# A hybrid decoder layer: the second x tile loaded in two parts, casts and two passes of squares moved to VectorE, and the order of k's and q's evacuations changed

## The chip, the cores and the metric

The kernel runs on one core of a Trainium2 chip. The metric is device time in microseconds (us) of one execution. The engines are named as in the profile: PE is TensorE's matmul (PEld its weight load), DVE is VectorE, ACT is ScalarE, POOL is GpSimd, SP is SyncE, which here only issues DMAs.

## What is computed

One layer of a decoder trunk on x of 1024 positions by 1024 channels, all in float32. What bears on the change is the head of it: the normalised input is projected to q, k and v, and q and k are normalised per head of 64 channels before a sliding-window attention.

```python
h = rmsnorm(x, mix_norm)                       # 1024 x 1024
q, k, v, su, sv, g_a, g_b = split(h @ w_in)    # q: 8 heads x 64; k, v: 2 heads x 64
q = rmsnorm(q, q_norm); k = rmsnorm(k, k_norm) # per head
scores = q @ k.T * 64 ** -0.5 + alibi          # window 128, blocks of 128 queries, sinks
y_att = softmax(scores) @ v
y_sgu = chunked_spatial_gating(su, sv, ...)
x = x + (sigmoid(g_a) * (y_att @ w_oa) + sigmoid(g_b) * (y_sgu @ w_ob)) @ w_out
x = x + conv_gated_mlp(rmsnorm(x, ffn_norm), ...)
```

## The kernel before

Every float32 product is made of three matmuls (`mm3`): each operand is split into a high part, rounded to TensorE's float32r, and a low part, the rest (`copy_hi` on ScalarE, then a subtraction on VectorE or GpSimd); high by high, high by low and low by high are summed in PSUM.

The head of the kernel, up to the first scores, is written out by hand: within `man = tc.manual_schedule()` each engine executes its instructions in the order of the program text, and TensorE does so throughout the kernel. Semaphores are put in by the framework. The stages are:

- A few matmuls of a tile of ones (`warm`, L230) keep TensorE busy while the first input arrives.
- `x_block(k)`, k = 0 to 7: x transposed comes from DRAM as eight tiles `xw[k]` of 128 channels by 1281 columns (one column of the norm's gain, 256 of k's and v's weights, 1024 positions). `xload` issues the loads on SP, tile 0 in two parts. ScalarE and VectorE write the high and low parts of the scaled positions (`x`, in halves of 512) and of the weights (`wkv`), and TensorE adds 24 matmuls to the two PSUM tiles `pkv`, which in the end hold k and v of all positions, positions on partitions.
- `wq_split(c)`: the weights of the first half of q's heads, two chunks of 128x1024, high part (L254) and low part (L255).
- `tsquare(t)`, t = 0 to 7: x comes a second time, by rows (`xt`, eight tiles of 128 positions by 1024 channels, `tload`), and the squares of each row are summed into column t of `ss8` (L219). All of `ss8` is needed for `eps_x` (L346) and `rstd` (L352), the reciprocal root of the rows' mean square. The input norm is so applied behind the projections; for q and k it drops out but for an epsilon, `eps_x`.
- `q_proj(n)`: 24 matmuls for 128 positions of four q heads, into a PSUM tile `pq` of pool H.
- Behind them: `q_sq`, squares of q; `q_ms`, their sums per head (L297, L298) and the power -1/2 on GpSimd (L299); `q_norm`, the product `qr` (L305); `q_trans`, two transposes on TensorE into `pqt` (L311); `q_split`, their high parts on ScalarE and low parts on VectorE (L320). For k: `ksq` and `kss` (L339, L340), `krs` (L347) and its power in two halves (L349, L403), `k_norm(h)`, the product `kr` (L356), `k_trans(h)`, four transposes into `pk` (L363), `k_hi` on ScalarE and `k_lo` on VectorE (L377) into kT, `k_twice`, a copy to the other half of the partitions. For v: `v_evac(h)` takes v out of `pkv` (L387), `v_split` splits it. `rms_rows` spreads `rstd` along rows by four matmuls with the identity (`rb`, L139) and copies it (`rstd_b`, L142).
- Then the attention: `s_mm(n)` makes the scores `sc` of 128 queries and four heads (L450, L453), `s_mask` adds the distance penalty (L466, L471), and TensorE is given other matmuls (`FILL`: later q groups, chunks of u and v of the gating unit) between.

Pool H has four PSUM tiles for `warm`, `pq`, `pk`, `pqt`, `rb` and later ones. A new tile takes the buffer whose last reader comes first in program order among those given back, and TensorE waits for that reader. The scores and `pkv` share another pool of two.

Of the kernel before, what the change touches and what calls it, by code (L numbers as in the profile page):

```python
# [13 lines left out]
AF = mybir.ActivationFunctionType  # L14
ALU = mybir.AluOpType
# [18 lines left out]
def build(tc, a):  # L34
    nc = tc.nc
    ctx = ExitStack()
    with ctx, tc.manual_schedule(engines={mybir.EngineType.PE}):
        body(ctx, tc, nc, a)


def body(ctx, tc, nc, a):
# [8 lines left out]
    def nm(s):  # L50
        uid[0] += 1
        return f"{s}_{uid[0]}"
# [15 lines left out]
    def Z(s, dt, shape, off=16):  # L68

        return late_by(zr[0], "Z", s, dt, shape, off)  # L70
# [8 lines left out]
    def PH(s):  # L79
        if psum.get("H") is None:  # L80
            return PS(s)[:, 0:512]
        return psum["H"].tile([128, 512], F, tag="H", name=nm(s))
# [4 lines left out]
    def copy_hi(dst, src, scale=1.0):  # L87
        return nc.scalar.activation(dst, src, AF.Copy, scale=scale)  # L88

    def mm3(out, wh, wl, mh, ml, first, last, **kw):  # L90

        nc.tensor.matmul(out, wh, mh, start=first, stop=False, **kw)  # L92
        nc.tensor.matmul(out, wh, ml, start=False, stop=False, **kw)  # L93
        nc.tensor.matmul(out, wl, mh, start=False, stop=last, **kw)  # L94
# [23 lines left out]
    mh05 = base.tile([128, 8], F, name="mh05")  # L118
    rstd = base.tile([128, 8], F, name="rstd")
# [14 lines left out]
    def rms_rows(pb, col, hs=(0, 1)):  # L134

        for h, p in zip(hs, pb):
            for s in range(4):
                c = 4 * h + s
                nc.tensor.matmul(p[:, s * 128:(s + 1) * 128], col[:, c:c + 1].to_broadcast([128, 128]), ident,  # L139
                                 start=True, stop=True)  # L140
        for h, p in zip(hs, pb):
            nc.scalar.copy(rstd_b[:, h * 512:(h + 1) * 512], p)  # L142
# [16 lines left out]
    wq = [Z("wq", R, (128, 2, 8, 256), 0)]  # L159
# [18 lines left out]
    def hx(j, k, c):  # L178

        h = c.start // 512  # L180
        return xq[k // 4][h][:, j, k % 4, c.start - 512 * h:c.stop - 512 * h]
# [14 lines left out]
    ss8 = at.tile([128, 8], F, name="ss8")  # L196
    pkv = [PS("pkv"), PS("pkv")]
    pk4 = [pkv[h].rearrange("p (s c) -> p s c", c=256) for h in range(2)]
    xr = {}
    x_first = [Y("xf", F, [128, 3, 1281]) for _ in range(2)]  # L200

    def xload(k):
        xr[k] = x_first[k // 3][:, k % 3, :] if k < 6 else pa.tile([128, 1281], F, tag="xr", name=nm("xr"), bufs=3)
        if k == 0:
            nc.sync.dma_start(xr[k][:, 0:513], a["xw"][k, :, 0:513])
            nc.sync.dma_start(xr[k][:, 513:1281], a["xw"][k, :, 513:1281])
        else:
            nc.sync.dma_start(xr[k], a["xw"][k])

# [6 lines left out]

    def tsquare(t):
        v = xt[t // 4][:, t % 4, :]
        nc.scalar.activation(v, v, AF.Square, accum_out=ss8[:, t:t + 1])  # L219

    man = tc.manual_schedule()
# [4 lines left out]
    nc.sync.dma_start(ident, a["ident"])  # L226
    nc.sync.dma_start(cp, a["cp"])
    warm = [PH("warm") for _ in range(4)]
    for i in range(11):
        nc.tensor.matmul(warm[i % 4][:, 0:128], rstd_b[:, 0:128], rstd_b[:, 0:128], start=True, stop=True)  # L230
    xcuts = {0: (slice(0, 256), slice(256, 512), slice(512, 1024))}

# [18 lines left out]
    def wq_split(c):  # L251
        rv = rwq[c].rearrange("p (k a) b -> p k (a b)", a=2)
        ks = slice(4 * c, 4 * c + 4)
        nc.scalar.activation(wq[0][:, 0, ks, :], rv, AF.Copy)  # L254
        nc.vector.tensor_tensor(wq[0][:, 1, ks, :], rv, wq[0][:, 0, ks, :].bitcast(F), op=ALU.subtract)  # L255

    x_block(0)
# [11 lines left out]
    x_block(7)  # L269
    wq_split(0)  # L270
    tsquare(0)
    tsquare(1)
    wq_split(1)
    for t in range(2, 6):
        tsquare(t)

    st = {}

    def q_proj(n):
        half, b = divmod(n, 8)  # L280
        w = wq[half]
        p = PH("pq")[:, 0:256]
        c = slice(b * 128, (b + 1) * 128)
        for k in range(8):
            mm3(p, hx(0, k, c), hx(1, k, c), w[:, 0, k, :], w[:, 1, k, :], k == 0, k == 7)
        st[("pq", n)] = p


    def q_sq(n):
        p = st.pop(("pq", n)).rearrange("p (h d) -> p h d", d=64)  # L290
        sq = qp.tile([128, 4, 64], F, tag="qsq", name=nm("qsq"), bufs=2)
        nc.scalar.activation(sq, p, AF.Square)
        st[("q", n)] = [p, sq]

    def q_ms(n):
        ss = qp.tile([128, 4], F, tag="qss", name=nm("qss"), bufs=4)
        nc.vector.tensor_reduce(ss, st[("q", n)][1], axis=AX.X, op=ALU.add)  # L297
        nc.vector.tensor_scalar(ss, ss, 1.0 / 64, eps_x[:, n % 8:n % 8 + 1], op0=ALU.mult, op1=ALU.add)  # L298
        nc.gpsimd.tensor_tensor(ss, ss, mh05[:, :4], op=ALU.pow)  # L299
        st[("q", n)][1] = ss  # L300

    def q_norm(n):
        p, ss = st.pop(("q", n))
        qr = st[("qr", n)] = qp.tile([128, 4, 64], F, tag="qr", name=nm("qr"), bufs=2)
        nc.vector.tensor_tensor(qr, p, ss.unsqueeze(2).to_broadcast([128, 4, 64]), op=ALU.mult)  # L305

    def q_trans(n):
        qr = st.pop(("qr", n)).rearrange("p h d -> p (h d)")
        p = PH("pqt")[:, 0:256]
        for t in range(2):  # L310
            nc.tensor.transpose(p[:, t * 128:(t + 1) * 128], qr[:, t * 128:(t + 1) * 128], ident)  # L311
        st[("qT", n)] = p

    def q_split(n):
        p = st.pop(("qT", n))
        qs = qp.tile([128, 2, 256], R, tag="qs", name=nm("qs"), bufs=2)
        for g in range(2):
            copy_hi(qs[ROWS[g], g, :], p[ROWS[g], :])
        for g in range(2):
            nc.vector.tensor_tensor(qs[ROWS[1 - g], g, :], p[ROWS[g], :], qs[ROWS[g], g, :].bitcast(F),  # L320
                                    op=ALU.subtract)
        st[("qT", n)] = qs
# [5 lines left out]
    krs = pa.tile([128, 16], F, name="krs")  # L328
# [3 lines left out]

    q_proj(0)
    q_proj(1)
    q_proj(2)
    ksqs = pa.tile([128, 8, 128], F, tag="sq", name="ksq")
    for h in range(2):
        ksq = ksqs[:, 4 * h:4 * h + 4, :]
# [1 line left out]
        nc.vector.tensor_reduce(kss[:, 8 * h:8 * h + 8], ksq.rearrange("p s (g d) -> p (s g) d", d=64),  # L340
                                axis=AX.X, op=ALU.add)
    tsquare(6)
    tsquare(7)
    nc.vector.tensor_scalar(kgq, cp[:, 184:185], cp[:, 185:186], -0.125, op0=ALU.mult, op1=ALU.mult)
    q_sq(0)
    nc.vector.tensor_scalar(eps_x, ss8, EPS / D, EPS * EPS, op0=ALU.mult, op1=ALU.add)  # L346
# [1 line left out]
                                   op0=ALU.mult, op1=ALU.add)  # L348
# [5 lines left out]
    def k_norm(h):  # L354
        ss = slice(4 * h, 4 * h + 4)
        nc.vector.tensor_tensor(kr[:, ss, :].rearrange("p s (g d) -> p s g d", d=64),  # L356
                                pk4[h][:, :, 0:128].rearrange("p s (g d) -> p s g d", d=64),
                                krs3[:, ss].unsqueeze(3).to_broadcast([128, 4, 2, 64]), op=ALU.mult)

    def k_trans(h):  # L360
        pk = PH("pk")
        for s in range(4):
            nc.tensor.transpose(pk[:, s * 128:(s + 1) * 128], kr[:, 4 * h + s, :], ident)  # L363
        st[("pk", h)] = pk

    def k_hi(h):
        cs = slice(512 * h, 512 * h + 512)
        pk = st[("pk", h)]
        for g in range(2):
            copy_hi(kTh[ROWS[g], g, cs], pk[ROWS[g], :], scale=kgq[ROWS[g], 0:1])  # L370

    def k_lo(h):
        cs = slice(512 * h, 512 * h + 512)
        pk = st.pop(("pk", h))
        for g in range(2):
            r = ROWS[g]
            nc.vector.scalar_tensor_tensor(kTl[r, g, cs], pk[r, :], kgq[r, 0:1], kTh[r, g, cs].bitcast(F),  # L377
                                           op0=ALU.mult, op1=ALU.subtract)

    def k_twice(h):  # L380
        cs = slice(512 * h, 512 * h + 512)
        for g in range(2):
            nc.scalar.copy(kTh[ROWS[1 - g], g, cs], kTh[ROWS[g], g, cs].bitcast(F))

    def v_evac(h):
        ss = slice(4 * h, 4 * h + 4)
        nc.vector.tensor_tensor(vt[:, ss, :], pk4[h][:, :, 128:256],  # L387
                                rstd[:, ss].unsqueeze(2).to_broadcast([128, 4, 128]), op=ALU.mult)

    def v_split():  # L390

        for g in range(2):
# [2 lines left out]
            copy_hi(vh_, vg_)  # L395
            nc.vector.tensor_tensor(vl_, vg_, vh_.bitcast(F), op=ALU.subtract)

    k_norm(0)
    k_trans(0)
    q_ms(1)  # L400
    q_norm(0)
    q_trans(0)
    nc.gpsimd.tensor_tensor(krs[:, 8:16], krs[:, 8:16], mh05, op=ALU.pow)  # L403
    q_norm(1)
    q_proj(3)
    q_sq(2)
    q_ms(2)
    nc.gpsimd.tensor_tensor(rstd, rstd, mh05, op=ALU.pow)
    nc.vector.tensor_scalar(nsink, sink_b, -1.0, None, op0=ALU.mult)
    k_hi(0)  # L410
    k_norm(1)
    q_split(0)
    k_lo(0)
    q_norm(2)
    q_trans(1)
    k_twice(0)
    rms_rows([PH("rb")], rstd, (0,))
    k_trans(1)
    q_sq(3)
    q_ms(3)  # L420
    v_evac(0)
    v_evac(1)
    copy_hi(u_next[0], u_raw[0])
    nc.gpsimd.tensor_tensor(u_next[1], u_raw[0], u_next[0].bitcast(F), op=ALU.subtract)
    q_split(1)
    rms_rows([PH("rb")], rstd, (1,))
    k_hi(1)
    k_lo(1)
# [1626 lines left out]
```

## Time and profile before

| what | us |
|---|---|
| median of 3 runs | 1177.23 |
| lowest and highest of them | 1176.56, 1178.11 |
| profiled execution | 1177.21 |
| span of its instructions | 1175.5 |
| TensorE busy in it | 1165.1 |
| first matmul of the first x block | 5.33 |
| first matmul of the first q group | 28.94 |
| first scores | 46.35 |

Times in the profile count from the start of the span. A timeline row gives the start, the duration of the merged group, engine, line and operation, the tile written and those read, shapes, the count, and in brackets the idle time of the engine ahead of it with what ended it. Where several instructions are merged (x2), the duration runs from the first start to the last end; neighbours on one engine overlap by up to 0.1 us. A row of the waits gives who waited for whom: us in total, times, longest. Lines are those of the kernel as printed above.

### The profile page before, as it was taken

The page shows a single profiled execution, that of the slowest core. Times are in us where ns is not written, and L with a number is a line of the kernel's source. Part 1 is how long each engine was busy: PE and PEld are TensorE (multiplying, and loading weights), DVE is VectorE, ACT ScalarE, POOL GpSimd, SP SyncE. Part 2 cuts the span into 40 slices and gives each one's busy share as a digit, 9 for nine tenths or more (in the row PEclk, how much of TensorE's full clock was granted, in tenths as well). Part 3 has the DMA queues.
Part 4 walks back from the last instruction along what each step waited for, and adds up shares of the span by engine and source line. Part 5 has one row for each costly group of instructions (what it writes and reads, how often), then busy time and mean ns, then how long its engine had stood idle before and what let it go on. Part 6 is the DMA issues. An engine that isn't in the chain of part 4 may idle for free.

```text
span 1175.5 us, 15803 instructions
## 1 busy us (share of the span) xinstructions
PE 1165.1 (99%) x5834; PEld 987.4 (84%) x5834; DVE 843.6 (72%) x974; ACT 565.5 (48%) x874; POOL 628.5 (53%) x434
## 2 busy tenths in 40 slices
PE   9999999999999999999999999999999999999998
PEld 9899999888888878888888888888888888888887
DVE  6677756743536876778788777887888787875674
ACT  7766568643436643334544444434444455425231
POOL 1567684598883863554877767676767640000000
PEclk9999999999999999999999999999999999999999
DMA  9210156256646763554554545454545268966471
GB/s 363 91 55 20 54 171 207 83 186 198 197 107 237 242 203 107 180 152 125 143 151 145 137 137 165 135 158 119 170 131 164 81 212 293 365 222 197 160 231 66
DMA packets 82093, 192.84 MB, mean 164 GB/s; under 512 B 9312, under 2 KB 16992, under 8 KB 81888
## 3 DMA queue, kind: packets, MB, share of 16 engines
q1 hardware_dynamic: 74160, 171.78, 42.3%
q0 software_dynamic: 7456, 15.73, 8.4%
q10 hardware_dynamic: 400, 4.33, 1.1%
q8 instruction: 46, 0.75, 0.3%
q14 instruction: 31, 0.25, 0.1%
HBM read 151.17 MB, written 49.02 MB: 170 GB/s over the span
## 4 chain that ended last, share of the span: by engine, by line
PE 85%; DVE 4%; ACT 3%; DMA 3%; POOL 2%; issue 1%; SPq 0%; DVEq 0%; POOLq 0%; ACTq 0%
PE pz L1068 48%; PE pd L1863 10%; PE pdy L1863 8%; PE px L94 2%; PE px L93 2%; PE px L92 2%; PE pu L94 1%; PE pu L92 1%; PE pu L93 1%; PE pv L525 1%; DMA xf<-xw 1%; PE pq L92 1%; PE pq L94 1%; PE pq L93 1%; DMA xt<-xt 1%
## 5 line engine op out<-in xcount | busy, mean ns | idle before, releaser
L1068 PE MATMUL pz<-T,qh 128*128 128x512 f32 x472 | 145.6, 390 | 0.0
L1068 PE MATMUL pz<-B,ph 128*128 128x512 f32 x352 | 109.6, 392 | 0.1
L1068 PEld LDWEIGHTS pz<-T,qh 128*128 128x128 f32 x472 | 88.4, 188 | 18.7 <-ACT u L893 0.3
L1027 POOL TENSOR_TENSOR pl<-lp,ph 128x1024 fp32r<-128x1024 f32 x30 | 75.2, 2505 | 53.1 <-ACT ph L88 53.1
L1068 PE MATMUL pz<-T,ql 128*128 128x512 f32 x236 | 91.8, 389 | 0.0
L1027 POOL TENSOR_TENSOR ql<-lq,qh 128x1024 fp32r<-128x1024 f32 x30 | 76.8, 2560 | 9.1 <-ACT qh L88 9.1
L1068 PEld LDWEIGHTS pz<-B,ph 128*128 128x128 f32 x352 | 65.2, 188 | 15.9 <-ACT x L1703 2.8
L1086 DVE TENSOR_TENSOR pz<-pz,rstd_b 128x1024 f32<-128x1024 f32 x60 | 73.9, 1232 | 4.5 <-ACT rstd_b L142 2.5
L1068 PE MATMUL pz<-T,s3h 128*128 128x512 f32 x232 | 71.4, 389 | 0.0
L1068 PE MATMUL pz<-y,wjh 128*128 128x512 f32 x224 | 69.5, 391 | 0.6 <-POOL y L1241 0.3
L1068 PE MATMUL pz<-B,pl 128*128 128x512 f32 x176 | 68.6, 390 | 0.0
L1863 PE MATMUL pd<-bh,ah 128*128 128x512 f32 x176 | 68.5, 389 | 0.0
L1863 PE MATMUL pd<-bl,ah 128*128 128x512 f32 x176 | 68.5, 389 | 0.0
L1863 PE MATMUL pd<-bh,al 128*128 128x512 f32 x176 | 68.5, 389 | 0.0
L1068 PE MATMUL pz<-B,AX 128*128 128x512 f32 x264 | 63.4, 389 | 0.0
L1068 PE MATMUL pz<-T,AX 128*128 128x512 f32 x264 | 63.4, 389 | 0.0
L1027 POOL TENSOR_TENSOR s3l<-lq,s3h 128x512 fp32r<-128x512 f32 x20 | 25.9, 1296 | 61.4 <-ACT s3h L88 61.4
L1068 PEld LDWEIGHTS pz<-T,AX 128*128 128x128 f32 x264 | 49.5, 188 | 10.3
L1068 PEld LDWEIGHTS pz<-B,AX 128*128 128x128 f32 x264 | 49.5, 188 | 10.3
L88 ACT ACTIVATE AX<-lr 128x1024 fp32r<-128x1024 f32 x22 | 23.4, 1064 | 69.9 <-POOL lr L629 69.9
L1558 DVE SCALAR_TENSOR_TENSOR tg<-pz,cp,tg 128x1023 f32<-128x1023 f32 (+1 forms) x44 | 56.3, 1278 | 0.8
L1558 DVE SCALAR_TENSOR_TENSOR tv<-pz,cp,tv 128x1023 f32<-128x1023 f32 (+1 forms) x44 | 56.2, 1278 | 0.8
(351 smaller groups left out, 3520.9 us busy)
## 6 DMA issues: line engine op xcount, KB each, us to landing
lp<-wup SPq DMA_DIRECT2D x22, 512.0 KB, 3.7
lq<-wup SPq DMA_DIRECT2D x22, 512.0 KB, 4.2
ra<-wdown SPq DMA_DIRECT2D x44, 256.0 KB, 4.8
b<-T SPq DMA_DIRECT2D x44, 256.0 KB, 3.7
lq<-wup POOLq DMA_DIRECT2D x42, 256.0 KB, 5.3
B<-tv SPq DMA_DIRECT2D x33, 256.0 KB, 2.1
T<-tt SPq DMA_DIRECT2D x33, 256.0 KB, 2.2
b<-B SPq DMA_DIRECT2D x33, 256.0 KB, 3.8
```

The costliest lines, as they stand in the source:

```text
L88: return nc.scalar.activation(dst, src, AF.Copy, scale=scale)
L92: nc.tensor.matmul(out, wh, mh, start=first, stop=False, **kw)
L93: nc.tensor.matmul(out, wh, ml, start=False, stop=False, **kw)
L94: nc.tensor.matmul(out, wl, mh, start=False, stop=last, **kw)
L525: nc.tensor.matmul(o, vhl[:, kb, g, :], w[:, 2 * g:2 * g + 2, :], start=i == 0 and g == 0, stop=i == len(ops) - 1, skip_group_check=True)
L1027: nc.gpsimd.tensor_tensor(l, r, h.bitcast(F), op=ALU.subtract)
L1068: nc.tensor.matmul(o, p[:, k, :], m, start=not more and k == 0 and j == 0, stop=k == nk - 1 and j == 2, skip_group_check=True)
L1086: nc.vector.tensor_tensor(z, z, rstd_b, op=ALU.mult)
L1558: nc.vector.scalar_tensor_tensor(t[:, j:], p[:, 0:1024 - j], cw[:, ci, 2 - j:3 - j], t[:, j:], op0=ALU.mult, op1=ALU.add)
L1863: nc.tensor.matmul(o[d], p[:, k - k0, m], q[:, k - k0, :], start=new and k == 0 and j == 0, stop=k == HK - 1 and j == 2, skip_group_check= ...
```

## The change

The second x tile is loaded in two parts, one with the gain, the weights and the first 512 positions, one with the rest. One warm matmul of eleven goes. The squares of row tiles 5 and 7 are taken by one `tensor_tensor_reduce` each on VectorE; the one of tile 7 stands right behind those of tiles 2 to 5 in program order, ahead of k's squares. The high part of q's weights is copied by VectorE. `q_proj(2)` goes behind `k_trans(0)`. The power of the second half of `krs` goes ahead of `k_norm(0)`, and so ahead of the power of `q_ms(1)`; that of `rstd` goes from behind `q_ms(2)` to behind `k_hi(0)`. `k_norm(1)`, `q_norm(1)`, both q transposes and `k_lo(0)` come ahead of `q_proj(3)`; `k_twice(0)`, both `v_evac`, `q_split(0)` and `q_split(1)` come ahead of `k_trans(1)` and of the first `rms_rows`, and so ahead of `q_ms(3)`.

```diff
         elif k == 1:
+            nc.sync.dma_start(xr[k][:, 0:769], a["xw"][k, :, 0:769])
+            nc.sync.dma_start(xr[k][:, 769:1281], a["xw"][k, :, 769:1281])
...
     def tsquare(t):
         v = xt[t // 4][:, t % 4, :]
+        if t in (5, 7):
+            nc.vector.tensor_tensor_reduce(out=v, in0=v, in1=v, scale=1.0, scalar=0.0, op0=ALU.mult, op1=ALU.add,
+                                           accum_out=ss8[:, t:t + 1])
+            return
         nc.scalar.activation(v, v, AF.Square, accum_out=ss8[:, t:t + 1])
...
-    for i in range(11):
+    for i in range(10):
         nc.tensor.matmul(warm[i % 4][:, 0:128], rstd_b[:, 0:128], rstd_b[:, 0:128], start=True, stop=True)
...
-        nc.scalar.activation(wq[0][:, 0, ks, :], rv, AF.Copy)
+        nc.vector.tensor_copy(wq[0][:, 0, ks, :], rv)
...
     for t in range(2, 6):
         tsquare(t)
+    tsquare(7)
...
     q_proj(0)
     q_proj(1)
-    q_proj(2)
...
     tsquare(6)
-    tsquare(7)
...
+    nc.gpsimd.tensor_tensor(krs[:, 8:16], krs[:, 8:16], mh05, op=ALU.pow)
     k_norm(0)
     k_trans(0)
+    q_proj(2)
     q_ms(1)
     q_norm(0)
+    k_hi(0)
+    nc.gpsimd.tensor_tensor(rstd, rstd, mh05, op=ALU.pow)
+    k_norm(1)
+    q_norm(1)
     q_trans(0)
-    nc.gpsimd.tensor_tensor(krs[:, 8:16], krs[:, 8:16], mh05, op=ALU.pow)
-    q_norm(1)
+    q_trans(1)
+    k_lo(0)
     q_proj(3)
     q_sq(2)
     q_ms(2)
-    nc.gpsimd.tensor_tensor(rstd, rstd, mh05, op=ALU.pow)
+    k_twice(0)
+    v_evac(0)
+    v_evac(1)
+    q_split(0)
+    q_norm(2)
+    q_split(1)
     nc.vector.tensor_scalar(nsink, sink_b, -1.0, None, op0=ALU.mult)
-    k_hi(0)
-    k_norm(1)
-    q_split(0)
-    k_lo(0)
-    q_norm(2)
-    q_trans(1)
-    k_twice(0)
+    k_trans(1)
     rms_rows([PH("rb")], rstd, (0,))
-    k_trans(1)
     q_sq(3)
     q_ms(3)
-    v_evac(0)
-    v_evac(1)
     copy_hi(u_next[0], u_raw[0])
     nc.gpsimd.tensor_tensor(u_next[1], u_raw[0], u_next[0].bitcast(F), op=ALU.subtract)
-    q_split(1)
     rms_rows([PH("rb")], rstd, (1,))
```

More of the change, by code (lines that the diff above doesn't have):

```diff
@@ L206, in xload @@
             nc.sync.dma_start(xr[k][:, 513:1281], a["xw"][k, :, 513:1281])
+        elif k == 1:
+            nc.sync.dma_start(xr[k][:, 0:769], a["xw"][k, :, 0:769])
+            nc.sync.dma_start(xr[k][:, 769:1281], a["xw"][k, :, 769:1281])
         else:
```

## The prediction

> **What bounds the kernel now.** I read the page first, then the waits of TensorE in the first 110 us, then each engine's timeline there, because the change touches nothing behind the first 50 us.
>
> ```profile
> span 1175.5 us, 15803 instructions
> PE 1165.1 (99%) x5834; PEld 987.4 (84%) x5834; DVE 843.6 (72%) x974; ACT 565.5 (48%) x874; POOL 628.5 (53%) x434
> ```
>
> TensorE is idle for only 1175.5 - 1165.1 = 10.4 us, so this is all that any reordering could win. The waits say where it lies at the start:
>
> ```profile
> PE rb L139 <- DVE kT L377: 1.1, 1, 1.1
> ...
> PE pkv L92 <- ACT x L88: 0.8, 1, 0.8
> PE pq L92 <- DVE qr L305: 0.6, 1, 0.6
> PE sc L450 <- DVE vt L387: 0.4, 1, 0.4
> PE sc L450 <- DVE sm L488: 0.3, 1, 0.3
> PE rb L139 <- ACT rstd_b L142: 0.3, 1, 0.3
> PE pkv L94 <- DVE x L243: 0.3, 1, 0.3
> ```
>
> Two places: 0.8 + 0.3 = 1.1 us in the second x block (pkv), and 1.1 + 0.6 + 0.4 + 0.3 = 2.4 us between the q groups and the first scores (sc). From the first scores on TensorE is nearly always fed, so the time of those scores (46.35) and of the third ones (57.58, the sc wait of 0.3) carries over into the end.
>
> **The x tile in two parts, one warm matmul fewer.**
>
> ```profile
> 9.94 0.42 ACT L88 ACTIVATE wkv<-xf 128x256 fp32r<-128x256 f32 x1 [0.28 <-DMA xf<-xw]
> 11.01 1.41 DVE L243 SCALAR_TENSOR_TENSOR x<-xf,x 128x512 fp32r<-128x512 f32 x2
> 10.00 0.38 PE L94 MATMUL pkv<-wkv,x 128*128 128x256 f32 x1 [0.28 <-DVE x L243]
> 28.94 0.28 PE L92 MATMUL pq<-wq,x 128*128 128x256 f32 x1
> ```
>
> From 10.00 to 28.94 TensorE runs without a gap, a matmul each 0.113 us, so block 2's third matmul stood at about 12.85. Its low part comes from the third tile, which lands at 9.9 whatever is done to the second, and is written by half of the 1.41 us row, 11.01 to 11.75. So the first q group can come forward by at most 12.85 - 11.8 = 1.05 us, to 27.9, and by nothing if the first part of the tile lands with the second. The warm matmul that goes (0.2 to 0.4 us by the clock rows below) is inside that bound, since block 2 waits for its tile either way. The extra issue on SP takes as long as the 0.43 us issue row of the next part and is hidden by the transfers: ScalarE still waited for the third tile at 9.94, 7 us after SP had issued the first, so the link is behind and not SP; were it not, every tile would come 0.4 later and the gain be 0.6. All of this counts only if TensorE sets the pace up to the scores, and the next part says that it doesn't.
>
> **Squares and casts moved.** These rows set the start of the normalisation, eps_x:
>
> ```profile
> 21.89 0.43 SPq L215 DMA_DIRECT2D xt<-xt  x1
> ...
> DMA to landing us min/median/max: 9.9/9.9/9.9
> 32.28 1.06 ACT L219 ACTIVATE xt<-xt 128x1024 f32<-128x1024 f32 x1
> 30.90 1.28 DVE L340 TENSOR_REDUCE kss<-ksq 128x8 f32<-128x512 f32 x2 [3.43 <-ACT ksq L339]
> 33.45 0.17 DVE L346 TENSOR_SCALAR eps_x<-ss 128x8 f32<-128x8 f32 x1 [1.16 <-ACT xt L219]
> 21.63 1.22 DVE L255 TENSOR_TENSOR wq<-wq,wq 128x1024 fp32r<-128x1024 f32 x1
> ```
>
> The last x row tile lands at 21.89 + 9.9 = 31.8. Now ScalarE squares it at 32.28, while VectorE has long reduced k's squares (30.90), so eps_x starts at 33.45. After the change VectorE squares it, and in program order this pass stands ahead of k's two reductions. VectorE works in that order, so the reductions wait for a transfer: 31.8, plus the square, plus 1.28 for the reductions, plus 0.1 for kgq. The square is an operation that the trace doesn't have; the same shape with two inputs took 1.22 (L255), and I take 1.2, with the overlap of neighbours. A 128x512 pass takes 0.69 (kr, below), so 512 columns are 0.53 and the floor for 1024 is 1.06; the upper end is 1.22 + 1.06 = 2.28, half rate. A gain is excluded, as the transfer's end is later than both reductions were before. eps_x then starts at about 34.25: **0.8 us later** (0.65 to 1.9). The other moved work, xt5's square and the two high parts of wq (at most 1.22 each, 3.7 in all), lies between 21.6 and 30.5, where the rows show VectorE with two instructions of 1.22 and a wait of 3.4; wq would be split by 21.6 + 4 x 1.22 = 26.5, ahead of q0 at 27.9. Without that cover q0 would start later by what is missing, and the 3.75 us stand that follows would swallow it. ScalarE is freed of as much, but in a stretch in which it would then wait for x rows: it gains nothing for the end.
>
> **The new order behind eps_x.** Durations:
>
> ```profile
> 33.92 1.68 POOL L349 TENSOR_TENSOR krs<-krs,mh 128x8 f32<-128x8 f32 x1 [30.21 <-DVE krs L347]
> 35.58 1.00 POOL L299 TENSOR_TENSOR qss<-qss,mh 128x4 f32<-128x4 f32 x1
> 40.54 1.64 POOL L408 TENSOR_TENSOR rstd<-rstd,mh 128x8 f32<-128x8 f32 x1
> 35.63 0.69 DVE L356 TENSOR_TENSOR kr<-pkv,krs 128x512 f32<-128x512 f32 x1 [1.13 <-POOL krs L349]
> 38.03 0.42 DVE L305 TENSOR_TENSOR qr<-pq,qss 128x256 f32<-128x256 f32 x1 [0.79 <-POOL qss L299]
> 40.34 0.86 DVE L320 TENSOR_TENSOR qs<-pqt,qs 64x256 fp32r<-64x256 f32 x2
> 41.23 1.51 DVE L377 SCALAR_TENSOR_TENSOR kT<-pk,kgq,kT 64x512 fp32r<-64x512 f32 x2
> 45.61 1.28 DVE L387 TENSOR_TENSOR vt<-pkv,rstd 128x512 f32<-128x512 f32 x2
> 38.51 0.38 PE L92 MATMUL pq<-wq,x 128*128 128x256 f32 x1 [0.59 <-DVE qr L305]
> 41.36 0.40 PE L311 MATMUL pqt<-ident,qr 128*128 128x128 f32 x2
> 44.75 1.16 PE L139 MATMUL rb<-ident,rstd 128*128 128x128 f32 x8 [0.29 <-ACT rstd_b L142]
> 46.35 0.51 PE L450 MATMUL sc<-kT,qs 128*128 128x256 f32 x2 [0.44 <-DVE vt L387]
> ```
>
> GpSimd: the first krs power (1.68) runs 34.7 to 36.4, qss of group 0 to 37.4. The second krs power is now ahead of group 1's qss: to 39.0, then qss to 40.0, rstd (1.64, as krs) to 41.6.
>
> TensorE: the groups q0 and q1 are 24 matmuls each, 2.72 us, and end at 27.9 + 5.44 = 33.35. Then come k's transposes, which need kr: 36.4 + 0.7 = 37.15. Before, q2 filled this time; now **TensorE stands for 3.75 us**, and q2 runs behind it, 37.7 to 40.4. The transposes of q0 and q1 follow, the second waiting for qr at 40.0 + 0.45. q3 needs a PSUM buffer: four are held by k's transposes, q2 and the two q transposes, and the first that program order gives back is k's, by k_lo(0). VectorE reaches k_lo(0) behind qr, 40.5 to 42.0. So q3 runs 42.05 to 44.9 (2.85, from 38.51 to 41.36 in the rows).
>
> VectorE meanwhile: q2's sums (0.6) to 42.6, v's two evacuations (1.28) to 43.85, q_split(0) to 44.7, q2's qr to 45.1, q_split(1) to 45.95. These give back the buffers for k's second transposes (44.9), the first rb (45.3) and the second (46.3). The v wait of 0.4 ahead of the scores is gone, since both evacuations end at 43.85; late next are these same rb matmuls, about 1.0 us each. The first scores start at 47.25, **0.9 us later** than 46.35, although q0 began 1.05 us sooner.
>
> The rb rows are also copied by ScalarE, and what follows there feeds the softmax:
>
> ```profile
> 44.11 0.58 ACT L142 COPY rstd_b<-rb 128x512 f32<-128x512 f32 x1 [2.89 <-PE rb L139]
> 45.97 0.75 ACT L88 ACTIVATE qs<-pqt 64x256 fp32r<-64x256 f32 x2
> 46.75 0.59 ACT L142 COPY rstd_b<-rb 128x512 f32<-128x512 f32 x1
> 56.74 0.69 DVE L471 TENSOR_TENSOR c<-sc,ali 128x512 f32<-128x512 f32 x1
> 57.58 0.47 PE L450 MATMUL sc<-kT,qs 128*128 128x256 f32 x2 [0.32 <-DVE sm L488]
> ```
>
> The first rb now stands behind q3 and k's second transposes, so its copy moves from 44.11 to 46.5, 2.4 later. Between it and the second copy q_split(1)'s two ScalarE passes (0.75) are gone, so the second copy is 1.65 later, and with it k_hi(1), k_lo(1), v's split, and the mask additions of the first two blocks, each waiting for the one before. The addition at 56.74 ends near 59.1 instead of 57.43. The third scores, which waited for it already, start at about 59.2: **1.65 us later**. Moving q_split(1) and the evacuations forward is worth the 0.75 that is counted here.
>
> **The sum.** The profiled execution took 1177.21 us, 1.7 over its span, and the median is 1177.23, so nothing is to be corrected: 1177.2 + 1.65 = **1178.9 us**. Of the 1.65, 0.8 is eps_x and 0.85 the order behind it. Ends: the square at its floor and the 0.85 caught by slack, +0.65, 1177.9; the square at half rate, +2.75, 1180.0. A change of 0.2%, 2.35 us, is about what can be told from none, so I forecast no change, a little on the slow side.
>
> **Rivals.**
>
> Slower by the clock. TensorE's first passes, started cold, were slow though the granted clock is 1.00 there:
>
> ```profile
> 2.50 1.49 PE L230 MATMUL warm<-rstd_b 128*128 128x128 f32 x6
> 2.00:4.50 2.50, 2.50 (x14) 2.50 (x13) 0.55 (x2) 0.90 (x3) 1.62 (x3) 1.00 0.88 317
> ```
>
> (The last row's columns are the stretch, its length, the busy time of each engine, the granted clock 1.00, DMA.) Six passes start (1.49 - 0.42) / 5 = 0.21 us apart; a pass of the same form in the rb row takes (1.16 - 0.28) / 7 = 0.13 or less, so slow is some 1.7 to 1.9 times longer. If the stand of 3.75 us before k's transposes brings the slow state back, q2's 24 matmuls take 4.6 to 5.1 instead of 2.7. Of the 1.9 to 2.4 lost 1.2 lie beside the wait for k_lo(0) (40.85 to 42.05); the rest, 0.7 to 1.2, goes to the end: 1179.6 to 1180.1, and it decides as soon as the loss passes that 1.2. Against it: no idle stretch in this trace is that long, so it shows neither. [...]
>
> Slower by the square. If an accumulating pass over two float inputs runs at half rate, it takes the 2.28 of the upper end and eps_x comes 1.1 later still: 1180.0. For it: nothing in the trace accumulates on VectorE. Against it: scalar_tensor_tensor with two float SBUF inputs took 0.7 per 512 columns (x, 1.41 for two), the full rate of the kr row. [...]
>
> Faster. TensorE's pace decides after all: eps_x is not what everything hangs on, the 1.05 of the x block comes through and the 2.4 of stalls shrink to nothing: 1177.2 - 3.45 = 1173.8. It needs kr by 33.35, when q1 ends; the x row that lands at 31.8 and 1.68 + 0.69 behind it speak against.
>
> Nothing: VectorE's reductions escape the wait, eps_x starts at 33.1, and the rest of the order costs its 0.85: 1178.0, no change either.
>
> **Chances.** Forecast 0.60, nothing 0.08, slow clock 0.12, half-rate square 0.12, faster 0.08. Slower by over 0.2% are both slow rivals and a sliver of the forecast (0.04): 0.28; faster 0.08; same 0.64. The range leaves out the faster case alone: it reaches from 1176.4, just under the fastest run shown (1176.56), to 1180.9, past both slow cases (1180.1 and 1180.0) by the 0.7 that single runs scatter.
>
> **What would show it.** The square of xt7 on VectorE at 31.8, k's reductions at 33.0, eps_x near 34.25; a TensorE wait of 3 to 4 us before pk on kr (1.68 of it GpSimd's power); q3 waiting about 1.2 for k_lo(0); first scores near 47.25, third near 59.2; the pkv waits down from 1.1 to 0.3 to 0.9. Slow clock: q2's matmuls 0.21 apart. I am wrong if eps_x starts before 33.5, or if scores stand before 46.35: then what I read as program order on VectorE, or the buffer that q3 waits for, was wrong.

## The result and the profile after

The changed kernel takes 1179.98 us (median of 22 executions, 1177.71 to 1186.58), the kernel before beside it 1177.55 (22, 1176.50 to 1180.17). The ratio is 1.0022, with a 95% interval of 1.0014 to 1.0031: slower, by about 2.4 us, with the estimate right at the bound of 0.2% below which the forecast called it no change. The forecast was 1178.9, inside a range of 1176.4 to 1180.9.

The profiled execution took 1181.49, 1.5 above the median; its span and engines, from the page:

```profile
span 1179.8 us, 15803 instructions
PE 1167.4 (99%) x5832; PEld 989.7 (84%) x5832; DVE 848.3 (72%) x980; ACT 561.7 (48%) x868; POOL 628.8 (53%) x434
```

TensorE is *busy* for 2.3 us more than the 1165.1 of before, though it has 2 matmuls fewer in the record. Work that is the same and takes longer points at its clock. The waits of TensorE in the first 110 us, to be held against the seven rows of before:

```profile
PE pk L369 <- DVE kr L362: 4.0, 1, 4.0
...
PE sc L457 <- DVE sm L495: 0.9, 1, 0.9
PE pk L369 <- DVE qs L328: 0.3, 1, 0.3
```

The many short waits have become one of 4.0 us, the stand of the forecast (a stretch without a matmul), where k's transposes wait for `kr`. Behind it, the windows of TensorE (stretch, length, busy time and matmuls, granted clock, DMA share and GB/s):

```profile
34.00:36.00 2.00, 0.00 (x0) 0.97 0.22 86
36.00:38.00 2.00, 1.28 (x6) 0.50 0.00 0
38.00:40.00 2.00, 2.00 (x12) 0.50 0.02 4
40.00:42.00 2.00, 2.00 (x11) 0.50 0.00 0
42.00:44.00 2.00, 2.00 (x17) 0.82 0.00 0
```

The kernel before shows 1.00 in each of these windows, for example:

```profile
36.00:38.00 2.00, 1.93 (x18) 1.00 0.01 4
```

In windows of a quarter of a microsecond the changed kernel's clock reads 1.00 or 0.50, and something between only at the two edges. So the mean of a longer window says when the clock changed: 0.97 means that it fell at 34 + 1.88 = 35.88, and 0.82 that it came back at 42 + 0.72 = 42.72. So **TensorE ran at half its clock for 6.84 us**, which covers k's first transposes and all of q2.

VectorE and GpSimd ahead of it, the rows that answer to L340, L346 and L356 of before:

```profile
31.35 1.22 DVE L223 CUSTOM_DVE_ANT_0 xt<-xt 128x1024 f32<-128x1024 f32 x1 [1.30 <-DMA xt<-xt]
32.50 0.08 DVE L223 DVE_READ_ACCUMULATOR2_ANT ss<- 128x1 f32 x1
32.50 1.27 DVE L347 TENSOR_REDUCE kss<-ksq 128x8 f32<-128x512 f32 x2
33.81 0.16 DVE L352 TENSOR_SCALAR eps_x<-ss 128x8 f32<-128x8 f32 x1
34.27 1.67 POOL L355 TENSOR_TENSOR krs<-krs,mh 128x8 f32<-128x8 f32 x1 [30.56 <-DVE krs L353]
35.97 0.69 DVE L362 TENSOR_TENSOR kr<-pkv,krs 128x512 f32<-128x512 f32 x1 [1.12 <-POOL krs L355]
```

The square of xt7 stands ahead of k's reductions and waits for its transfer, as the forecast read it; eps_x starts 0.36 later than before. Then the timeline of TensorE:

```profile
27.16 0.28 PE L92 MATMUL pq<-wq,x 128*128 128x256 f32 x1
36.72 1.12 PE L369 MATMUL pk<-ident,kr 128*128 128x128 f32 x4 [3.96 <-DVE kr L362]
37.49 0.56 PE L92 MATMUL pq<-wq,x 128*128 128x256 f32 x1
42.74 0.60 PE L319 MATMUL pqt<-ident,qr 128*128 128x128 f32 x4
43.10 0.37 PE L92 MATMUL pq<-wq,x 128*128 128x256 f32 x1
48.63 0.36 PE L457 MATMUL sc<-kT,qs 128*128 128x256 f32 x1
60.69 0.47 PE L457 MATMUL sc<-kT,qs 128*128 128x256 f32 x2 [0.88 <-DVE sm L495]
```

The first q group starts 1.78 us sooner than before (27.16 for 28.94) and is done at 36.72 - 3.96 = 32.76. From there the lead is lost: q2 takes 42.74 - 37.49 = 5.25 us for its 24 matmuls, 0.21 each and not 0.113. The first scores start 2.3 us later than before, the third ones 3.1 later.

The mean clock of the whole execution was below 1.000 in 20 of the 22 executions of the changed kernel (0.998 or less in 15), and in 17 of 77 executions of the kernel before that were run with the experiments (0.998 or less in one). A mean of 0.999 need not come from the head: in the profiles of e1 and e4 below, at 0.999, the clock is 1.00 in every window from 30 to 80, and the changed kernel's own falls once more in its last 4.5 us (0.95). The changed kernel's two executions at 1.000 took 1177.71 and 1178.20, some 2 us less than its median.

### The profile page after: what moved, and what is told of

It reads as the page before. It is cut to its first block, busy times and chain, and to the rows that moved or that the text cites. A ratio compares the mean times of both kernels' runs of the same rounds, so it can differ in the third digit from the quotient of the medians.

```text
span 1179.8 us, 15803 instructions
## 1 busy us (share of the span) xinstructions
PE 1167.4 (99%) x5832; PEld 989.7 (84%) x5832; DVE 848.3 (72%) x980; ACT 561.7 (48%) x868; POOL 628.8 (53%) x434
## 4 chain that ended last, share of the span: by engine, by line
PE 86%; DVE 2%; ACT 2%; POOL 2%; issue 1%; DMA 1%; SPq 0%; DVEq 0%; ACTq 0%; POOLq 0%
PE pz L1075 50%; PE pd L1870 10%; PE pdy L1870 8%; PE px L94 2%; PE px L92 2%; PE px L93 2%; PE pv L532 1%; PE pu L94 1%; PE pu L92 1%; PE pu L93 1%; PE pq L92 1%; PE pq L94 1%; PE pq L93 1%; DMA wj<-wb 1%; PE pt L502 1%
```

## The experiments

All were timed in five rounds against the kernel before. Edits are to the changed kernel where nothing else is said. In short: e1 and e5 fill the stand, e2 and e6 put q2 back ahead of k's transposes, e3, e8, e9 and e10 place the square of xt7, e4 is the split alone, e7 the order alone, and in e11 v's evacuations come earlier. Each was profiled once. Three starts, read in each profile, carry the argument: eps_x, the first scores and the third scores. The columns in the middle are their differences, and the last two the time and the ratio to the kernel before.

| kernel | eps_x | to first scores | to third scores | third start | median us | ratio, 95% |
|---|---|---|---|---|---|---|
| before | 33.45 | 12.90 | 11.23 | 57.58 | | |
| changed | 33.81 | 14.82 | 12.06 | 60.69 | 1179.98 | 1.0022 (1.0014, 1.0031) |
| e1 | 33.03 | 12.88 | 12.06 | 57.97 | 1180.77 | 1.0030 (1.0020, 1.0041) |
| e2 | 34.14 | 15.17 | 12.11 | 61.42 | 1183.23 | 1.0046 (1.0034, 1.0059) |
| e3 | 33.58 | 13.67 | 12.06 | 59.31 | 1177.74 | 1.0002 (0.9993, 1.0011) |
| e4 | 33.13 | 12.89 | 11.23 | 57.25 | 1177.55 | 1.0000 (0.9991, 1.0009) |
| e5 | 33.30 | 12.87 | 12.06 | 58.23 | 1178.52 | 1.0006 (0.9997, 1.0015) |
| e6 | 33.77 | 15.41 | 12.12 | 61.30 | 1182.35 | 1.0034 (1.0021, 1.0046) |
| e7 | 33.06 | 12.89 | 12.06 | 58.01 | 1181.02 | 1.0024 (1.0013, 1.0034) |
| e8 | 32.01 | 12.90 | 11.23 | 56.14 | 1176.17 | 0.9987 (0.9978, 0.9996) |
| e9 | 33.16 | 12.89 | 11.24 | 57.29 | 1177.24 | 1.0002 (0.9993, 1.0011) |
| e10 | 32.58 | 12.91 | 12.06 | 57.55 | 1177.98 | 1.0005 (0.9996, 1.0014) |
| e11 | 33.09 | 13.49 | 11.66 | 58.24 | 1176.69 | 0.9994 (0.9985, 1.0002) |

The second column is 12.9 wherever the clock stayed at 1.00, with either order, and longer in exactly the profiles in which it fell (changed, e2, e3, e6, e11). The third is 11.23 with the old order (11.66 in e11, where the slow clock lasted past the first scores) and 12.06 to 12.12 with the new one. The kernel before had a median of 1177.55 beside the changed kernel, 1177.30 beside e1 to e4, 1177.67 beside e5 to e8 and 1177.48 beside e9 to e11.

**e1 and e5: filling the stand.** The theory: the clock falls because TensorE stands; a few matmuls without effect keep it up. The rival: the slow matmuls are hidden by the wait for `k_lo(0)`, and filling changes nothing. Both fill with 14 matmuls of the tile of ones; e1 gives them a PSUM tile of their own, e5 writes them into the tile that k's transposes then overwrite.

```diff
     k_norm(0)
+    dum = PH("dum")                                       # e1
+    for i in range(14):
+        nc.tensor.matmul(dum[:, 0:128], rstd_b[:, 0:128], rstd_b[:, 0:128], start=True, stop=True)
     k_trans(0)
...
         pk = PH("pk")                                     # e5, in k_trans
+        for i in range(14 if h == 0 else 0):
+            nc.tensor.matmul(pk[:, 0:128], rstd_b[:, 0:128], rstd_b[:, 0:128], start=True, stop=True)
```

> The changed kernel with 14 matmuls of the tile of ones put ahead of k's first transposes, so that TensorE works (about 14 x 0.23 = 3.2 us) while it would stand. They are issued where nothing else could run, and no other work is moved. If the slow clock behind the stand is what costs: granted clock 1.00 throughout, q2's matmuls 0.113 us apart, q3 again bound by k_lo(0) at about 41.4, first scores near 46.6 and third near 58.6 (48.6 and 60.7 in the changed kernel), time about 1178.5, some 2 us under the changed kernel and 1 over the kernel before. If the order behind eps_x costs by itself (PSUM buffers, ScalarE's chain of copies), the time stays within 0.7 us of the changed kernel's, clock or not.

> The changed kernel with the 14 filling matmuls again, but written into the PSUM buffer that k's first transposes then overwrite, so that every later tile has the buffer it has in the changed kernel. The first filled run took a buffer more, and TensorE waited 1.6 us for VectorE at 215 us, where the changed kernel doesn't wait. If that wait came from the shifted buffers, it is gone here, the granted clock stays 1.00, and what is left is the order behind eps_x: third scores 0.4 to 1.0 us later than before, time 1177.8 to 1178.3, 2 us under the changed kernel. If the late wait comes back, or the fill itself costs, 1180 or more.

In both the clock is 1.00 through the head and the first scores come 12.9 behind eps_x. In e5 the wait for `k_lo(0)` stands where the forecast had it; from its timeline:

```profile
36.27 0.60 PE L371 MATMUL pk<-ident,kr 128*128 128x128 f32 x4
36.63 0.37 PE L92 MATMUL pq<-wq,x 128*128 128x256 f32 x1
39.45 0.60 PE L319 MATMUL pqt<-ident,qr 128*128 128x128 f32 x4
41.02 0.36 PE L92 MATMUL pq<-wq,x 128*128 128x256 f32 x1 [0.96 <-DVE kT L385]
```

From k's transposes to q3 it is 41.02 - 36.27 = 4.75 us, against 43.10 - 36.72 = 6.38 in the changed kernel. The median falls to 1178.52, a little above the 1178.3 expected and 0.85 above the kernel before beside it (1177.67), where the changed kernel was 2.43 above. So the clock costs 1.9 us (14.82 - 12.90) at the first scores and about 1.6 at the end; the second figure is uncertain by some 1.5 us, as each ratio is by 0.9 per mille, but the changed kernel's two executions at 1.000 say much the same.

e1 has the better start and yet ends at 1180.77, later than the changed kernel and outside both its expectations. Its waits further on hold one that neither the kernel before nor the changed one has, at 215 us, in the gating products of the layer:

```profile
PE pz L1078 <- DVE vg L778: 1.6, 1, 1.6
```

**e2 and e6: q2 back ahead of k's transposes, the rest as changed.** With work in the stand, the clock should stay up.

```diff
     k_norm(0)
-    k_trans(0)
+    pk0 = PH("pk")                 # e6 alone: the tiles are taken in the changed kernel's order
     q_proj(2)
+    k_trans(0)                     # e6: k_trans(0, pk0)
```

> The changed kernel with q_proj(2) back ahead of k's first transposes, all else as changed. If the stand costs by its clock alone: the wait ahead of pk falls from 4.0 to about 1.1 us, but TensorE then has little to do until k_lo(0) frees q3's buffer at 41.4, so q3 and all behind it stand where the run with filled-in matmuls has them: about 1178.5. If the clock goes by the share of work and not by one unbroken stand, q3 runs slow here and the time is 1180 or more. If q2's place is all that is wrong with the change, the time is that of the kernel before or less, 1177.0.

> The changed kernel with q_proj(2) ahead of k's first transposes, the transposes' PSUM buffer taken before q2's, so that all buffers stay as in the changed kernel. In the first run of this edit no wait was over 2 us, yet the clock fell at 41.2, and a late wait of 1.6 us came as in the first filled run. If buffers made the late wait: it is gone and the time is 1181.6, 1.6 under the first run, still over the changed kernel's 1180, as the slow clock then covers q3 and the transposes behind it. If the late wait was only the later schedule, 1183 again.

The clock fell all the same, later. For e2, at 1183.23, that is the second case of its expectation; e6's 1182.35 lies between its two. Of e2, its waits in the first 110 us and its windows:

```profile
PE pqt L319 <- DVE qr L313: 2.2, 2, 1.9
PE pk L369 <- DVE kr L362: 1.1, 1, 1.1
...
PE pq L92 <- DVE kT L383: 0.8, 1, 0.8
```

```profile
36.00:38.00 2.00, 0.69 (x5) 1.00 0.01 4
38.00:40.00 2.00, 0.41 (x2) 1.00 0.00 0
40.00:42.00 2.00, 0.82 (x3) 0.60 0.01 4
42.00:44.00 2.00, 2.00 (x10) 0.50 0.00 0
44.00:46.00 2.00, 2.00 (x11) 0.50 0.00 0
46.00:48.00 2.00, 2.00 (x15) 0.70 0.00 0
```

No stand here is longer than 1.9 us (the 2.2 are two waits); but between 36 and 40 TensorE is busy for 1.1 of 4 us, since `q_trans(1)` ahead of q3 makes it wait for VectorE. Windows read as above, the clock falls at 40.4 and is back at 47.2: 6.8 us again. So it isn't one long stand that counts, a stretch with little work does it too. Both have the wait of 1.6 near 215 us as well; e6 was to take it away by handing out these tiles in the changed kernel's order, and didn't.

**e7: the new order alone, on the kernel before.**

```diff
-    q_proj(2)
...
+    nc.gpsimd.tensor_tensor(krs[:, 8:16], krs[:, 8:16], mh05, op=ALU.pow)
     k_norm(0)
     k_trans(0)
+    q_proj(2)
...  (and the rest of the order as in the change)
```

> The kernel before with the new order alone: q_proj(2) behind k's first transposes and everything from k_norm(0) on as in the changed kernel; one x tile in one part, all squares and casts on ScalarE, eleven warm matmuls. eps_x stays at 33.45, q1 ends at 34.4 and kr at 36.0, so TensorE stands only 1.7 us. By my sum the order alone costs 0.85, through ScalarE's first rb copy: third scores at 58.4, time 1178.1. If the slow clock comes after such a stand too, 1179.5 or more. If the order gains, because no tile waits for evacuations, 1176.5.

From eps_x to the scores it did what was expected: q1 ends later there, the stand is only 1.8, the clock stays at 1.00, and the third scores start 0.43 late, at an eps_x 0.39 earlier than before, which was to stay. The time missed, 1181.02. The two longest of the late waits in its list that the kernel before lacks add up to 2.1 us, and with the 0.43 to 2.5 of the 3.35 by which it is slower:

```profile
PE pz L1068 <- DVE vg L768: 1.6, 1, 1.6
PE pv L525 <- POOL cl L513: 0.5, 1, 0.5
```

**e4: the split of the x tile alone, on the kernel before.**

> The kernel before with the second x tile loaded in two parts, and nothing else of the change. The changed kernel's tiles all landed 0.4 to 1.1 us sooner. By the chain through the last row tile, eps_x comes 0.4 sooner and the time is 1177.1 (0.4 under the kernel before); the 1.1 us of TensorE's waits in the second x block that go are not to be seen in the end. If TensorE's pace counts there, 1176.4.

In the kernel before, ScalarE took the third tile's weights from 9.94; with the split alone, and in e7, where the second tile is loaded in one part as before:

```profile
8.95 0.42 ACT L88 ACTIVATE wkv<-xf 128x256 fp32r<-128x256 f32 x1 [0.88 <-DMA xf<-xw]
```

```profile
8.74 0.42 ACT L88 ACTIVATE wkv<-xf 128x256 fp32r<-128x256 f32 x1 [0.41 <-DMA xf<-xw]
```

So the tile *behind* the second one can land a microsecond sooner, with the split or without: it scatters by that much between executions, and that the split brings it sooner is not shown. In e4 q0 starts at 27.86 (28.33 in e7, 28.94 before). Eps_x and the third scores come 0.32 and 0.33 sooner, no more than e7's 0.39, but the end shows nothing above its uncertainty of 0.9 per mille: 1.08 us of TensorE time at q0 was hidden, as the forecast said.

**e3, e8, e9, e10: the place of the square.** In e3 the square of xt7 goes behind k's reductions.

```diff
-    tsquare(7)            # behind the squares of tiles 2 to 5
...
     tsquare(6)
+    tsquare(7)            # behind k's squares and their reductions
```

> The changed kernel with VectorE's square of the last row tile moved behind the two reductions of k's squares, nothing else. My theory has those reductions held up by that square: eps_x comes from 33.8 to about 32.6, TensorE's stand ahead of pk shrinks from 4.0 to about 2.6 us, too short for the clock to fall, and first scores come near 45.4, third near 57.4: time about 1177.2, as the kernel before. If the clock falls all the same, 1179. If the order on VectorE is not what holds eps_x, nothing moves: 1180.

It is as fast as the kernel before. But the stand was to be too short for the clock to fall, an estimate that no run had shown, and the clock falls too, for half as long; windows of e3:

```profile
34.00:36.00 2.00, 0.00 (x0) 1.00 0.28 113
36.00:38.00 2.00, 1.50 (x12) 0.91 0.03 10
38.00:40.00 2.00, 2.00 (x11) 0.50 0.01 4
40.00:42.00 2.00, 2.00 (x15) 0.74 0.00 0
```

0.91 and 0.74 put the fall at 37.64 and the return at 41.04, 3.4 us. Its stand was 3.0, and xt7 landed late in this profile (its square starts at 32.23). At 1178.44 it is the slowest of the 11 executions, and the row in the table is not typical of them.

e8 has the change's front (split, ten warm matmuls, casts and squares on VectorE) with the square last and the order of the kernel before; e9 is the same with the square in the changed kernel's place.

> The other half: x tile in two parts, ten warm matmuls, q's casts and two squares on VectorE, the last of them behind k's two reductions, and the order behind that as in the kernel before (q_proj(2) ahead of k's transposes). eps_x then follows the landing of the last row tile by 1.35 us, some 0.4 to 0.9 sooner than before (32.6 to 33.1), TensorE is busy until 35.8 and no clock falls: third scores 0.4 to 0.9 sooner, time 1176.6, a gain of 0.05%, if anything can be seen. If the landing of that tile scatters by more than is gained (30.6 to 32.2 in the runs so far), no difference.

> The whole front of the change (split tile, ten warm matmuls, casts and both squares on VectorE, xt7's square ahead of k's reductions) with the order of the kernel before behind it. Against e8 only the place of xt7's square differs, so this prices it. Theory (the square's place costs what eps_x comes later: square 1.22 and reductions 1.27 behind the landing at 30.7 to 31.7, against a square alone): eps_x 33.3 to 34.2, 0.7 to 1.2 later than e8's 32.01 for the same landing, third scores 57.2 to 58.1, time 1177.0 to 1177.8, the same as before; TensorE is fed by the third q group meanwhile, so the granted clock stays 1.00. Rival (the place is hidden, and e8 gained by the split and the casts): third scores about 56.2 and 1176.2, as e8. Rival 2 (a new order on VectorE brings the late wait of 1.6 near 215 us): 1178.5 or more.

VectorE in e8, then in e9:

```profile
29.27 1.27 DVE L347 TENSOR_REDUCE kss<-ksq 128x8 f32<-128x512 f32 x2
30.67 1.23 DVE L223 CUSTOM_DVE_ANT_0 xt<-xt 128x1024 f32<-128x1024 f32 x1
...
32.01 0.17 DVE L353 TENSOR_SCALAR eps_x<-ss 128x8 f32<-128x8 f32 x1
```

```profile
30.70 1.23 DVE L223 CUSTOM_DVE_ANT_0 xt<-xt 128x1024 f32<-128x1024 f32 x1 [1.31 <-DMA xt<-xt]
31.85 0.08 DVE L223 DVE_READ_ACCUMULATOR2_ANT ss<- 128x1 f32 x1
31.85 1.28 DVE L348 TENSOR_REDUCE kss<-ksq 128x8 f32<-128x512 f32 x2
...
33.16 0.17 DVE L353 TENSOR_SCALAR eps_x<-ss 128x8 f32<-128x8 f32 x1
```

The square starts at the same time in both (30.67, 30.70). So it is its place that moves eps_x, by 1.15, and the third scores follow by 1.15 and the median by 1.07 (1.26 against the kernel before beside each). In these profiles this prices the place by itself. **e8, at 0.9987 (0.9978 to 0.9996), beats both kernels**; its third scores come 1.44 sooner than before, as eps_x does, where 0.4 to 0.9 was expected.

> The changed kernel with xt7's square behind k's reductions (as e3) and 14 matmuls of a tile of ones filling the stand ahead of k's transposes (as e5); their output is overwritten by the transposes. Theory (three separate terms: clock, square's place, order): e5 lost 0.65 at the third scores with the square ahead; with it behind, eps_x is 0.7 to 1.2 earlier, so no drop of the clock, third scores 57.0 to 57.6, and 1177.0 to 1177.6, the same as before. Rival (the clock's drop in e3 cost nothing, as its 1177.74 was no slower than before): no better than e3, 1177.5 to 1178.0. Rival 2 (the late wait near 215 us appears): 1178.5 or more.

e10 is e3 with e5's filling, made to see whether the three terms add. Its third scores start at 57.55, as before and at the edge of what was expected; its time, 1177.98, is above the expected 1177.6, no better than e3, and its interval holds no change. At the scores the terms add, at the end they differ by less than can be measured here. The filling was too long for this stand, VectorE having written `kr` by 34.76 + 0.69 = 35.45, and cost the first scores nothing:

```profile
34.76 0.69 DVE L362 TENSOR_TENSOR kr<-pkv,krs 128x512 f32<-128x512 f32 x1 [1.13 <-POOL krs L355]
```

```profile
36.42 0.60 PE L371 MATMUL pk<-ident,kr 128*128 128x128 f32 x4
```

The first scores come 12.91 behind eps_x, as with the transposes on time: k's transposes had about a microsecond of slack in this order.

**e11: v's evacuations ahead of the second q transposes, on e8.**

> As e8, with both evacuations of v right behind k_lo(0), ahead of q_norm(2), the second q transposes and k_twice(0). Theory (the sc wait of 0.4 for vt is what stands last ahead of the first scores): that wait goes, first scores 44.5 instead of 44.9, and the time 1175.8, 0.3 to 0.4 under e8. Rival (VectorE's 1.28 for the evacuations now delays the product of the third q group and the reads that give back the buffer for the first rb, which already waited 1.1 for k_lo(0)): first scores 44.9 to 45.5, and 1176.2 to 1176.8.

The `vt` wait went, but k's second transposes then waited 0.7, and in this profile the clock fell:

```profile
42.00:44.00 2.00, 1.13 (x8) 1.00 0.00 0
44.00:46.00 2.00, 1.61 (x9) 0.68 0.04 8
46.00:48.00 2.00, 2.00 (x11) 0.50 0.00 0
48.00:50.00 2.00, 2.00 (x18) 0.96 0.15 18
```

from 44.72 to 48.16, 3.4 us, with no stand over 1.1. The median, 1176.69, lies in the rival's range, 0.5 above e8's, but the two intervals overlap, so that e11 is slower than e8 is not shown. The first scores, at 46.58, lie outside both ranges: eps_x came at 33.09, and the clock fell.

## Why the prediction came out so

At the third scores the profile of the changed kernel is 3.11 late: 0.36 by eps_x, 1.92 on the way to the first scores and 0.83 from there to the third. The forecast had 0.8, 0.1 and 0.75.

- **The wrong step is the chance of the slow clock.** The forecast named this rival, with its place and sign, and gave it 0.12. That chance was the author's estimate: the trace of before, with "no idle stretch" that long, could tell neither way. No run shows one so small: by the mean clock it came in 15 to 20 executions of 22. Nor does it take a stand of 3.75: e3 stood for 3.0, and e2 and e11 never for more than 1.9 and 1.1, and their clock fell.
- **Its price was also too small.** The forecast had 0.7 to 1.2: 1.9 to 2.4 of slow matmuls less the 1.2 hidden beside the wait for `k_lo(0)`. The upper end held: q2 lost 2.43 (5.25 against 2.82 in e5), and 1.21 was hidden, as forecast, since q3 starts 0.36 behind the start of q's transposes (43.10 - 42.74) and in e5 1.57 (41.02 - 39.45). Two terms were left out. k's transposes were slow as well (0.77 from the first to q2, against 0.36 in e5: 0.41). And from q3 to the first scores it takes 5.53 against 5.15 in e5, 0.38 more, of which 0.3 is the wait of k's second transposes for VectorE's split of q (`qs`). The sum, 2.43 - 1.21 + 0.41 + 0.38 = 2.0, is about the 1.95 by which the first scores follow eps_x later than in e5 (14.82 - 12.87).
- **The order's 0.85 was right.** It shows as 0.83 from the first to the third scores in every kernel with the new order (0.89 at most). The path was right too: the second copy of `rb` starts 13.30 behind eps_x before and in e8, and 14.12 to 14.15 in e5, e7 and e10. That e5's median is +0.85 as well proves little, as its interval holds no change. The forecast had put 0.1 of it ahead of the first scores; there is none of it there.
- **The eps_x term was right in mechanism, 0.8 for 0.36 in size.** From the start of the square to eps_x it takes 2.46 (31.35 to 33.81), for a forecast 2.45. The square's place costs 1.15 by itself (e8 against e9). The forecast kept the landing of the last x row at 31.8, and excluded a gain on that ground; the landing moves. The square starts behind it at 31.35 in the changed kernel, at 30.84 in e5 and at 30.70 in e9, and with e5's landing eps_x is 0.15 *sooner* than before. The profiles with the same front scatter so much that which part is due to the change can't be told from them.
- **The half-rate square is refuted**: 1.22 us, and 0.08 to read the sum, where the forecast took 1.2. No run shows the half rate, whose 2.28 us are in the forecast's +2.75: in e3, e5, e8 and e9 the square took 1.23.
- **Faster** was refuted in the form given: TensorE's gain at q0 was 1.78, more than the 1.05 bound, and none of it arrived. The bound failed since the third tile landed sooner too (8.79 for 9.94), which "lands at 9.9 whatever is done to the second" had ruled out; e7 has 8.74 with the second tile in one part, so how much of this is the split stays open. The pkv waits are not 0.3 to 0.9 but gone.
- **The stand** was 3.96 for a forecast 3.75, and q3's wait for `k_lo(0)` is hidden by the slow q2, but there in e5.

With the clock kept up, e5's 1178.5 lies close to the forecast's 1178.9, but in part by chance: its eps_x is 0.15 sooner and not 0.8 later than before, and its third scores 0.65 later and not 1.65. The result lay beyond it by a rival that should have been the likeliest. That 1179.98 still lies inside the range is luck as far as the forecast's own case goes, which did not come: the range had room for the slow rivals, and the clock's was priced at 1179.6 to 1180.1.

What stays open: the late wait of 1.6 in e1, e2, e6 and e7. It is on a VectorE result near 215 us in products that no edit touches. e5 and e7 have the same order ahead of the scores, and e5 doesn't have it. That another assignment of PSUM buffers makes these products wait is an inference; e6, made to undo it, didn't. And the last 1.2 us of the changed kernel's profiled execution (4.28 behind the one of before, 3.11 at the third scores) was not traced to an edit.

## What to carry to other kernels

When an order makes TensorE wait, count what its clock will do, not only the length of the wait: look for stretches of some 3 to 4 us in which it would do little (here every fall in the head followed 3.4 us in which it was busy for 0.3 to 1.5), whether in one stand or several, and either fill them or leave the order that fills them with real work. On an engine that executes in order, put what waits for a transfer behind what is ready: here one line's place was worth 1.1 us. And price a tail by differences between fixed marks (here eps_x, first and third scores), since they separate the terms where the total cannot.

## What was not expected of the hardware

- The granted clock fell to 0.50 about 3.1 us behind the last matmul (32.76 to 35.88), and stayed there 6.84, 3.4, 6.8 and 3.44 us in the changed kernel, e3, e2 and e11: one or two steps of 3.4, while TensorE was at work again. It was one step where TensorE was busy throughout it (e3, e11), and two where TensorE still stood in the first (until 36.72 in the changed kernel, and the wait of 0.8 for `kT` in e2).
- It can fall without a long stand. In the 3.4 us ahead of the fall, a stretch as long as one such step, TensorE was busy for 0.29 (changed), 1.1 (e2, e3), 1.2 (e6) and 1.54 (e11). In the profiles at 1.00 no stretch of 3.4 us between 26 and 50 us holds less than 1.56 (e7) or about 2.0 (before, e4, e8, e9). So these profiles fit a share of work of about 0.46 (1.54 and 1.56 of 3.4); e7 and e11 are too close to tell a bound from chance, and e11's own executions differ: 0.998 in three of 11, 1.000 in six.
- When a transfer lands scatters by a microsecond between executions: ScalarE took the third x tile's weights from 9.94 (before) and 8.74 (e7) with the second tile in one part, and with it in two VectorE began xt7's square, behind its landing, from 30.70 (e9) to 32.23 (e3).
